# One row group of an encoder kernel: a second turn of its rows in the rounded type, compared with the full turn

## The chip, the cores and the metric

The kernel runs on one core of one Trainium2 chip. The metric is the device time of one execution in microseconds (us), from the first to the last work of the core. Times of before are the median of three executions and their lowest and highest. One further execution was taken by the hardware profiler; it has a time of its own, and all durations below come from it.

## The reference, cut to what matters

Two sequences of 1024 rows of 1024 channels, `x_prompt` and `x_sample`, go through one layer and a last norm. All is in float32.

```python
h = rmsnorm(x, g_mix) * (1.0 + sc1) + sh1
z = h @ w_in
q_lat, kv_lat, k_pe, f_in = z[..., :o1], z[..., o1:o2], z[..., o2:o3], z[..., o3:]
y_mla = mla_group(q_lat, kv_lat, k_pe, ...)
y_four = fourier_group(f_in, w_four)
x = x + ga1 * (jnp.concatenate([y_mla, y_four], axis=-1) @ w_out)
h2 = rmsnorm(x, g_ffn) * (1.0 + sc2) + sh2
x = x + ga2 * ((jax.nn.silu(h2 @ w_gate) * (h2 @ w_up)) @ w_down)
```

What the change touches is the first of these lines: the normed rows `x`, turned so that channels lie on the 128 partitions, and then scaled and shifted into `h`.

## The kernel before

**Stages.** The first stage, up to about 215 us, norms the rows of both sequences, turns them, projects them (`z = h @ w_in`, the Fourier columns folded with the cosine and sine tables), and writes latents to DRAM. It also folds small weights on the side. Attention and the Fourier part come next, up to about 740 us, and the rest is the feed-forward layer. Products of float32 values are made on TensorE (PE) as three products of split values: a value is split into a high part of the type `fp32r` and a low part that is the rest (`split`, L61 to L63: the high part by a copy on ACT, the low part by a subtraction on DVE), and `mm3` (L82 to L85) adds high times high, high times low and low times high.

**Row groups.** The first stage goes over eight groups `k` (`pairs`, L364), four for each sequence; a group is two row tiles `u` of 128 rows, `st1["x", k]`, each 128 x 1024. For a group, `norm` squares and scales the rows in place (L381 on ACT, `rstd` on POOL, L393 on DVE). `flip(k, g)` for g = 0 to 3 turns two channel tiles of both row tiles: `flip_t` makes four transposes on PE against the float32 identity `ident` into one PSUM bank (L409), and `flip_s` scales and shifts the bank into `hf` (L421 on ACT for k of 2 and more) and splits `hf` into `hh` and `hl`. The products that read `hh` and `hl` of group k + 1 come only in the next round.

**The place of the change.** `pair(k)` (L695) is one round. In round 2 stand, in this order in the code: the products of group 2 with `wz` for row tile 0 (`zproj`), whose bank is squared, given its reciprocal root and scaled into a tile `lat` (L490, L491 on DVE), the last 128 columns of it split into the tile `kv` (ACT and DVE) and sent to DRAM by two DMAs on SP's queue (L496, `ckv_d`); then `flip(3, 0)` and `flip(3, 1)`; then a piece of side work (L245 folds a weight, L222 multiplies the conditioning vector with a 1 MB block `wada` that SP loads with L215); then `zproj` for row tile 1.

**What sets the order.** A scheduler places the instructions on each engine's queue once, when the program is built. Each engine then takes its queue in that order, and an instruction that waits holds up all behind it. SP issues nearly all DMAs of this stage, also in order. PSUM has eight banks that go round (`bank`, tag `b`), and the SBUF tiles of tag `sk` (`stile`, L187) are three.

Of the kernel before, what the change touches and what calls it, by code (L numbers as in the profile page):

```python
# [13 lines left out]
F32R = mybir.dt.float32r  # L14
BF16 = mybir.dt.bfloat16
AF = mybir.ActivationFunctionType
ALU = mybir.AluOpType
# [4 lines left out]
P = 128  # L22
# [30 lines left out]
def hybrid_encoder_kernel(ctx: ExitStack, tc: tile.TileContext, a: dict):  # L53
    nc = tc.nc
# [3 lines left out]
    def rd(t):  # L58
        return t.bitcast(F32)

    def split(hi, lo, src):  # L61
        here["a"] = nc.scalar.copy(hi, src).ins  # L62
        here["v"] = nc.vector.tensor_tensor(out=lo, in0=src, in1=rd(hi), op=ALU.subtract).ins  # L63
# [29 lines left out]
    identr = const.tile([P, P], F32R, name="identr")  # L93
# [81 lines left out]
    with ExitStack() as st:  # L175
        p1b = st.enter_context(ExitStack())
        w2 = p1b.enter_context(tc.tile_pool(name="p1b", bufs=1, side="right", reuse_waits="tile"))
        w = st.enter_context(tc.tile_pool(name="p1", bufs=1, reuse_waits="tile"))
        pp = st.enter_context(tc.tile_pool(name="p1_ps", bufs=8, space=PSUM, reuse_waits="tile"))

        def bank():
            return pp.tile([P, 512], F32, tag="b", name="bank")
# [4 lines left out]
        def stile(name):  # L187
            return w.tile([P, 512], F32, tag="sk", name=name, bufs=3)
# [176 lines left out]
        st1 = {}  # L365
# [28 lines left out]

        def flip(k, g):
            flip_t(k, g)
            flip_s(k, g)

        def flip_t(k, g):
            if g == 0:  # L400
                st1["hf", k] = w2.tile([P, NC, 2, P], F32, tag="hf", name="hf", bufs=1)
                st1["hh", k] = w.tile([P, NC, 2, P], F32R, tag=f"hh{k % 2}", name="hh")
                st1["hl", k] = w.tile([P, NC, 2, P], F32R, tag=f"hl{k % 2}", name="hl")
            xt = st1["x", k]
            pt = bank().rearrange("p (c u t) -> p c u t", c=2, u=2)
            for c in range(2):
                for u in range(2):
                    cc = 2 * g + c
                    here["pe"] = nc.tensor.transpose(pt[:, c, u, :], xt[u][:, cc * P : (cc + 1) * P], ident).ins  # L409
            st1["pt", k, g] = pt  # L410

        def flip_s(k, g):
            s, j = pairs[k]
            hf, pt = st1["hf", k], st1.pop(("pt", k, g))
            for c in range(2):
                cc = 2 * g + c
                sc, sh = s1[s][:, cc : cc + 1], sh1[s][:, cc : cc + 1]
                if k < 2 and c == 1:
                    nc.vector.tensor_scalar(out=hf[:, cc], in0=pt[:, c], scalar1=sc, scalar2=sh, op0=ALU.mult, op1=ALU.add)
                else:  # L420
                    nc.scalar.activation(hf[:, cc], pt[:, c], AF.Identity, bias=sh, scale=sc)  # L421
            gs = slice(2 * g, 2 * g + 2)
            split(st1["hh", k][:, gs], st1["hl", k][:, gs], hf[:, gs])
# [271 lines left out]
        def pair(k, also=None):  # L695
# [22 lines left out]
            if k < nk - 1:  # L718
                flip(k + 1, 0)
                flip(k + 1, 1)  # L720
# [6 lines left out]
            if k + 1 < nk:  # L727
                flip(k + 1, 2)
                flip(k + 1, 3)
# [164 lines left out]
    with ExitStack() as st:  # L894
        early = st.enter_context(ExitStack())
        wa = early.enter_context(tc.tile_pool(name="p2a", bufs=1, reuse_waits="tile"))
        w = st.enter_context(tc.tile_pool(name="p2", bufs=1, side="right", reuse_waits="tile"))
        pp = st.enter_context(tc.tile_pool(name="p2_ps", bufs=8, space=PSUM, reuse_waits="tile"))
# [174 lines left out]
        for s in range(2):  # L1073
            for n in range(8):
                g, j = n // 4, (1, 2, 3, 0)[n % 4]
# [100 lines left out]
    with ExitStack() as st:  # L1176
        w = st.enter_context(tc.tile_pool(name="p3", bufs=1, side="right", reuse_waits="tile"))
        pp = st.enter_context(tc.tile_pool(name="p3_ps", bufs=1, space=PSUM, reuse_waits="tile"))
# [112 lines left out]
        for k in range(nit + 4):  # L1291
# [7 lines left out]
            if k < nit:  # L1299
                s, b, h, u = items[k]  # L1300
# [34 lines left out]
    with ExitStack() as st:  # L1335
        w = st.enter_context(tc.tile_pool(name="p5", bufs=1, reuse_waits="tile"))
# [150 lines left out]
        pp = st.enter_context(tc.tile_pool(name="p5_ps", bufs=8, space=PSUM, reuse_waits="tile"))  # L1487
# [19 lines left out]
        for s in range(2):  # L1507
# [78 lines left out]
            for n, f in enumerate(order):  # L1586
# [55 lines left out]
                x, y, z = bank(), bank(), bank()  # L1642
# [332 lines left out]
```

## Time and profile before

| | |
|---|---|
| median of 3 executions | 2033.69 us (2029.91 to 2034.99) |
| the profiled execution's own time | 2032.84 us |
| its span, first to last instruction | 2031.1 us |
| time around the span | 1.74 us |
| mean granted TensorE clock | 0.995 of full speed |
| DMA over the span | 370.33 MB, mean 182 GB/s |

The profile names instructions by their line in the kernel and by tiles, output first. "x8" behind a row means eight such instructions in a row. A duration in a timeline is that of the whole merged row, and the bracket at its end gives the idle time of the engine before it and what ended it. Matmuls overlap one another, so the distance between the starts of rows says more of PE's pace than the durations. PEclk is the clock that TensorE was granted, 1.00 at full speed.

### The profile page before, as it was taken

What the parts mean: (1) busy time and instruction counts of PE and PEld (TensorE: products, weight loads), DVE (VectorE), ACT (ScalarE), POOL (GpSimd) and SP (SyncE); (2) the same over time, 40 slices, a digit from 0 to 9 for tenths busy, and PEclk for the clock granted to TensorE, in tenths of its full rate; (3) what the DMA queues carried; (4) which work ended last, traced back from release to release, by engine and by line L of the source; (5) the groups of instructions that cost most, each with busy time, mean ns of one, the idle gap of its engine ahead of it and who ended that gap; (6) DMA issues with size and microseconds to landing.
All of it is one profiled execution on the core that took longest, in us unless ns stands there. A gap on an engine that the chain in (4) does not pass through costs nothing.

```text
span 2031.1 us, 28284 instructions
## 1 busy us (share of the span) xinstructions
PE 1985.5 (98%) x9840; PEld 1621.9 (80%) x9840; DVE 1405.3 (69%) x2088; ACT 896.3 (44%) x1733; POOL 824.3 (41%) x1013
## 2 busy tenths in 40 slices
PE   8899999999999999999999999999999999999997
PEld 7788777888787777888888888877788888888876
DVE  5667658766676679878677577687765656657674
ACT  4565545555554564333333365453333333336451
POOL 2454112112213227879778411233655554510142
PEclk9999999999999999999999999999999999999999
DMA  9695883445544475555555597664422322357772
GB/s 377 209 292 171 264 329 109 121 99 139 130 115 145 136 263 188 201 166 194 200 171 193 170 310 249 215 233 145 141 93 102 116 93 103 113 188 265 230 225 90
DMA packets 181963, 370.33 MB, mean 182 GB/s; under 512 B 18556, under 2 KB 58236, under 8 KB 177724
## 3 DMA queue, kind: packets, MB, share of 16 engines
q1 hardware_dynamic: 163148, 310.71, 45.9%
q0 software_dynamic: 18672, 57.81, 9.5%
q8 instruction: 77, 1.26, 0.3%
q14 instruction: 66, 0.54, 0.1%
HBM read 256.46 MB, written 120.39 MB: 186 GB/s over the span
## 4 chain that ended last, share of the span: by engine, by line
PE 51%; DMA 3%; DVE 3%; issue 1%; POOL 1%; ACT 1%; SPq 1%; DVEq 0%; ACTq 0%; POOLq 0%
PE bank L84 17%; PE bank L83 17%; PE bank L85 17%; DVE wl L63 1%; DMA val<-x_d 1%; DMA H<-s_d 1%; ACT wh L62 1%; DMA draw<-s_d 1%; POOL val L143 1%; DVE val L143 1%; DMA draw<-t_d 0%; DVE val L1772 0%; SPq L1732 0%; SPq L1731 0%; POOL rs_y L110 0%
## 5 line engine op out<-in xcount | busy, mean ns | idle before, releaser
L83 PE MATMUL bank<-H,wh 128*128 128x512 f32 x1224 | 477.4, 390 | 5.4 <-DVE val L143 4.8
L85 PE MATMUL bank<-H,wl 128*128 128x512 f32 x1224 | 476.4, 389 | 0.2 <-DVE wl L63 0.2
L84 PE MATMUL bank<-H,wh 128*128 128x512 f32 x1224 | 476.3, 389 | 0.0
L143 DVE TENSOR_TENSOR val<-bank,val 128x512 f32<-128x512 f32 x244 | 166.6, 688 | 170.6 <-PE bank L85 167.7
L83 PEld LDWEIGHTS bank<-H,wh 128*128 128x128 f32 x1224 | 229.8, 188 | 56.7 <-DVE val L143 7.1
L85 PEld LDWEIGHTS bank<-H,wl 128*128 128x128 f32 x1224 | 229.8, 188 | 49.4 <-DVE wl L63 1.5
L84 PEld LDWEIGHTS bank<-H,wh 128*128 128x128 f32 x1224 | 229.8, 188 | 47.3
L63 DVE TENSOR_TENSOR wl<-draw,wh 128x512 fp32r<-128x512 f32 x286 | 201.2, 738 | 83.4 <-ACT wh L62 82.9
L62 ACT CAST wh<-draw 128x512 fp32r<-128x512 f32 x286 | 168.7, 620 | 159.5 <-PE bank L84 84.5
L84 PE MATMUL bank<-wl,wh 128*128 128x512 f32 x572 | 223.8, 391 | 3.1 <-DVE wl L63 2.7
L143 POOL TENSOR_TENSOR val<-val 128x512 f32<-128x512 f32 x58 | 82.6, 1431 | 347.8 <-DVE val L1746 188.8
L85 PE MATMUL bank<-wh,wl 128*128 128x512 f32 x572 | 222.6, 389 | 0.0
L83 PE MATMUL bank<-wh 128*128 128x512 f32 x572 | 222.6, 389 | 0.0
L62 ACT CAST wh<-rgu 128x512 fp32r<-128x512 f32 x171 | 106.3, 623 | 251.0 <-PE bank L84 196.0
L63 DVE TENSOR_TENSOR wl<-val,wh 128x512 fp32r<-128x512 f32 x133 | 134.1, 1010 | 74.4 <-ACT wh L62 74.4
L63 DVE TENSOR_TENSOR wl<-rgu,wh 128x512 fp32r<-128x512 f32 x171 | 164.1, 960 | 7.6 <-ACT wh L62 7.6
L62 ACT CAST wh<-val 128x512 fp32r<-128x512 f32 x133 | 82.3, 622 | 178.8 <-PE bank L84 162.9
L140 POOL TENSOR_TENSOR val<-rgu 128x512 f32<-128x512 f32 x80 | 113.3, 1417 | 97.5 <-DMA rgu<-in_wgu_dram 93.8
L84 PEld LDWEIGHTS bank<-wl,wh 128*128 128x128 f32 x572 | 107.4, 188 | 29.2 <-DVE wl L63 7.2
L83 PEld LDWEIGHTS bank<-wh 128*128 128x128 f32 x572 | 107.4, 188 | 22.4
L85 PEld LDWEIGHTS bank<-wh,wl 128*128 128x128 f32 x572 | 107.4, 188 | 22.0
L140 POOL TENSOR_TENSOR val<-val 128x512 f32<-128x512 f32 x89 | 119.2, 1358 | 1.3
(393 smaller groups left out, 3910.6 us busy)
## 6 DMA issues: line engine op xcount, KB each, us to landing
rgu<-in_wgu_dram SPq DMA_DIRECT2D x86, 512.0 KB
draw<-s_d SPq DMA_DIRECT2D x143, 256.0 KB
s_d<-val POOLq DMA_DIRECT2D x88, 256.0 KB, 3.8
draw<-t_d SPq DMA_DIRECT2D x88, 256.0 KB
s_d<-val SPq DMA_DIRECT2D x66, 256.0 KB
wada<-in_wa_dram SPq DMA_DIRECT2D x16, 1024.0 KB
draw<-in_w_down_dram SPq DMA_DIRECT2D x55, 256.0 KB
xt<-in_x_dram SPq DMA_DIRECT2D x16, 512.0 KB
```

The source lines that it names most:

```text
L62: here["a"] = nc.scalar.copy(hi, src).ins
L63: here["v"] = nc.vector.tensor_tensor(out=lo, in0=src, in1=rd(hi), op=ALU.subtract).ins
L83: nc.tensor.matmul(out, lh, rh, start=first, stop=False, skip_group_check=cont)
L84: nc.tensor.matmul(out, lh, rl, start=False, stop=False, skip_group_check=cont)
L85: here["pe"] = nc.tensor.matmul(out, ll, rh, start=False, stop=last, skip_group_check=cont).ins
L140: return eng.tensor_tensor(out=out, in0=x, in1=y, op=ALU.subtract).ins
L143: return eng.tensor_tensor(out=out, in0=x, in1=y, op=ALU.add).ins
```

## The change

`flip(3, 0)`, one of 24 calls of `flip`, does more between its transposes and its scaling. The parts of both row tiles that it turns (256 channels each) are copied by two DMAs into a tile `xr` of the type fp32r. Four transposes against `identr`, the identity in fp32r, turn `xr` into a second bank `pr`. DVE then copies `pr` into a tile `d`, subtracts the bank of the full turn, multiplies by 1048576 and adds the full turn again. `flip_s` reads `d` in the place of the bank. What is computed is therefore the full turn plus 1048576 times the difference between the two turns; where the fp32r turn hands on the same values, that is the full turn itself.

```diff
         def flip(k, g):
             flip_t(k, g)
+            if (k, g) == (3, 0):
+                xr = w.tile([P, 512], F32R, tag="sk", name="xr", bufs=3).rearrange("p (c u t) -> p c u t", c=2, u=2)
+                pr = pp.tile([P, 512], F32R, tag="b", name="pr").rearrange("p (c u t) -> p c u t", c=2, u=2)
+                for u in range(2):
+                    nc.sync.dma_start(rd(xr)[:, :, u, :], st1["x", k][u][:, : 2 * P].rearrange("p (c t) -> p c t", c=2))
+                for c in range(2):
+                    for u in range(2):
+                        nc.tensor.transpose(pr[:, c, u, :], xr[:, c, u, :], identr)
+                d = stile("d").rearrange("p (c u t) -> p c u t", c=2, u=2)
+                nc.vector.tensor_copy(d, rd(pr))
+                nc.vector.tensor_tensor(out=d, in0=d, in1=st1["pt", k, g], op=ALU.subtract)
+                nc.vector.tensor_scalar(out=d, in0=d, scalar1=1048576.0, scalar2=None, op0=ALU.mult)
+                nc.vector.tensor_tensor(out=d, in0=d, in1=st1["pt", k, g], op=ALU.add)
+                st1["pt", k, g] = d
             flip_s(k, g)
```

The lines behind the inserted ones carry numbers that are 14 higher: L409 becomes L423 and L496 becomes L510. The added lines are L401 (the DMAs), L404 (the transposes) and L406 to L409 (the four steps on DVE). The scheduler places them as follows. Outside of the first stage the order of all five engines is what it was.

PE's queue in round 2 of before, from the last product of `zproj` for row tile 0 on; `bank<-ident,xt` are the eight transposes of `flip(3, 0)` and `flip(3, 1)`, and the bracket names the semaphores that a row waits for:

```order
L85 MATMUL bank<-wz_h,hl 128x448
L409 MATMUL bank<-ident,xt 128x128 [waits DVE_49,PE_49]
L409 MATMUL bank<-ident,xt 128x128 [waits DVE_49]
L409 MATMUL bank<-ident,xt 128x128 x6
L245 MATMUL bank<-wukT,zraw 128x128 x2
L222 MATMUL bank<-wada,scT 32x512 [waits DMAHW6_49]
```

The same place of PE's queue in the change:

```order
L423 MATMUL bank<-ident,xt 128x128 [waits DVE_49,PE_49]
L423 MATMUL bank<-ident,xt 128x128 [waits DVE_49]
L423 MATMUL bank<-ident,xt 128x128 x2
L404 MATMUL pr<-identr,xr 128x128 [waits DMAHW0_49]
L423 MATMUL bank<-ident,xt 128x128
L404 MATMUL pr<-identr,xr 128x128 [waits DMAHW1_49]
L404 MATMUL pr<-identr,xr 128x128 x2
L423 MATMUL bank<-ident,xt 128x128 x3
L245 MATMUL bank<-wukT,zraw 128x128 [waits PE_49]
L245 MATMUL bank<-wukT,zraw 128x128
L222 MATMUL bank<-wada,scT 32x512 [waits DMAHW6_49]
```

The four new transposes stand in the midst of the eight old ones, behind the fourth and the fifth of them, and two of them wait for DMAs.

SP's queue at the same place of before: the two DMAs of `kv` of group 2, row tile 0, the store of a folded weight, the load of the next `wada`, and the `kv` of row tile 1:

```order
L496 DMA ckv_d_93<-kv 128x128 [waits DMAHW6_49,Activation_49]
L496 DMA ckv_d_94<-kv 128x128 [waits DMAHW7_49,DVE_49]
L251 DMA wq_d<-zraw 256x1x512 [waits DMAHW0_49]
L215 DMA wada<-in_wa_dram 128x2048 [waits DMAHW1_49,PE_49]
L496 DMA ckv_d_93<-kv 128x128 [waits DMAHW2_49,Activation_49]
```

And of the change:

```order
L510 DMA ckv_d_93<-kv 128x128 [waits DMAHW6_49,Activation_49]
L510 DMA ckv_d_94<-kv 128x128 [waits DMAHW7_49,DVE_49]
L401 DMA xr<-xt 128x2x128 [waits DMAHW0_49,Pool_49]
L401 DMA xr<-xt 128x2x128 [waits DMAHW1_49]
L215 DMA wada<-in_wa_dram 128x2048 [waits DMAHW2_49,PE_49]
L251 DMA wq_d<-zraw 256x1x512 [waits DMAHW3_49,DVE_49]
```

The two new DMAs stand right behind the pair of `kv`, and the load of `wada` and the store of the folded weight have changed places behind them.

DVE's queue of before there, from the scaling of `lat` on:

```order
L491 TENSOR_SCALAR lat<-bank,rs_r 128x128
L247 SCALAR_TENSOR_TENSOR zraw<-bank,vecs,gkvr 128x128 [waits PE_49]
L247 SCALAR_TENSOR_TENSOR zraw<-bank,vecs,gkvr 128x128
L63 TENSOR_TENSOR hl<-hf,hh 128x512 [waits Activation_49]
L63 TENSOR_TENSOR kv<-lat,kv 128x128 [waits DMAHW2_49,DMAHW1_49,Activation_49]
L63 TENSOR_TENSOR hl<-hf,hh 128x512 [waits Activation_49]
```

And of the change:

```order
L505 TENSOR_SCALAR lat<-bank,rs_r 128x128
L63 TENSOR_TENSOR kv<-lat,kv 128x128 [waits DMAHW2_49,DMAHW1_49,Activation_49]
L406 COPY d<-pr 128x512 [waits PE_49]
L407 TENSOR_TENSOR d<-d,bank 128x512 [waits DVE_49]
L408 TENSOR_SCALAR d<-d 128x512 [waits DVE_49]
L247 SCALAR_TENSOR_TENSOR zraw<-bank,vecs,gkvr 128x128 [waits PE_49]
L409 TENSOR_TENSOR d<-d,bank 128x512 [waits DVE_49]
L63 TENSOR_TENSOR hl<-hf,hh 128x512 [waits Activation_49]
```

The subtraction that makes `kv` has come forward to stand right behind `lat`, and the four new steps stand behind it.

## The prediction

> **What bounds the kernel now.** I read the page's head first, then TensorE's waits, then the busy time by stretches around the place of the change.
>
> ```profile
> span 2031.1 us, 28284 instructions
> ...
> PE 1985.5 (98%) x9840; PEld 1621.9 (80%) x9840; DVE 1405.3 (69%) x2088; ACT 896.3 (44%) x1733; POOL 824.3 (41%) x1013
> ```
>
> PE is busy for 98% of the span, and no other engine is near that. A share over the span says little of one place, so next come the stretches. The columns are the stretch, its length, the busy time of each engine, PEclk, the DMA share and GB/s.
>
> ```profile
> 93.00:101.00 8.00, 8.00 (x51) 6.58 (x50) 5.42 (x12) 4.88 (x15) 3.71 (x10) 1.00 0.65 250
> 101.00:108.00 7.00, 7.00 (x57) 5.02 (x55) 3.35 (x9) 6.34 (x18) 3.73 (x10) 1.00 0.89 294
> 108.00:130.00 22.00, 22.00 (x127) 18.97 (x128) 15.16 (x32) 13.35 (x33) 11.61 (x26) 1.00 0.88 286
> 130.00:230.00 100.00, 98.91 (x627) 85.67 (x626) 74.40 (x166) 56.72 (x148) 43.74 (x97) 1.00 0.65 204
> ```
>
> From 93 to 130 us PE has no idle time at all, and from 130 to 230 us it has 1.1 us. So work that is added to PE here, or a time in which PE waits here, has next to nothing in the following 137 us that could take it up. All else in the stage has room: DVE works 5.42 of 8 us, ACT 4.88.
>
> **The change part by part: the wait.** These are PE's rows at the place.
>
> ```profile
> 93.01 1.03 PE L409 MATMUL bank<-ident,xt 128*128 128x128 f32 x8
> 93.88 0.61 PE L245 MATMUL bank<-wukT,zraw 128*128 128x128 f32 x4
> 94.42 1.06 PE L222 MATMUL bank<-wada,scT 128*32 128x512 f32 x8
> 95.42 0.47 PE L83 MATMUL bank<-wz_h,hh 128*128 128x448 f32 x1
> ...
> 100.22 0.37 PE L85 MATMUL bank<-wz_h,hl 128*128 128x448 f32 x1
> ```
>
> The eight transposes of `flip(3, 0)` and `flip(3, 1)` start 0.11 us apart (0.87 us from the first to the next row), so the fourth is issued by 93.45 us. In the change the first transpose of `xr` is next, and it waits for a DMA that SP issues behind the two DMAs of `kv`. So the question is when `kv` of this row tile is ready.
>
> ```profile
> 96.58 0.48 DVE L490 TENSOR_SCALAR lat<-bank,rs_r 128x256 f32<-128x256 f32 x1 [1.79 <-POOL rs_r L114]
> 96.99 0.34 DVE L491 TENSOR_SCALAR lat<-bank,rs_r 128x128 f32<-128x128 f32 x1
> ...
> 98.36 1.38 DVE L63 TENSOR_TENSOR kv<-lat,kv 128x128 fp32r<-128x128 f32 x1
> 97.36 0.30 ACT L62 CAST kv<-lat 128x128 fp32r<-128x128 f32 x1 [1.14 <-DVE lat L491]
> 97.69 2.41 SPq L496 DMA_DIRECT2D ckv_d<-kv  x2
> 99.77 0.33 SPq L496 DMA_DIRECT2D ckv_d<-kv  x1
> L63 DVE TENSOR_TENSOR kv<-lat,kv x8: 278/444/1380, 62.2 to 128.7; 128x128 fp32r<-128x128 f32 x8
> ```
>
> The chain is the reciprocal root on POOL, `lat` on DVE until 97.33 us, the high part of `kv` on ACT until 97.66 us, and the low part on DVE. Nothing in it waits for what follows on PE, so it keeps its times while PE stands. The low part is made earlier than before, since it now stands right behind `lat`: 97.66 us and 0.28 us (the minimum of eight; its 1.38 us here is the longest) are 97.94 us. The second `ckv_d` is then issued at about 98.0 us instead of 99.77, the first DMA of `xr` after its 0.33 us at 98.4, and the second, after 0.5 us, at 98.9.
>
> No row shows a copy of this kind from issue to landing. The nearest is the second `ckv_d` itself, half as large; the other end is the page's row for a store of 256 KB.
>
> ```profile
> 99.50:100.40 0.90, 0.90 (x6) 0.80 (x5) 0.84 (x2) 0.00 (x0) 0.09 (x1) 1.00 0.00 0
> 100.40:101.00 0.60, 0.60 (x7) 0.57 (x6) 0.00 (x0) 0.37 (x3) 0.00 (x0) 1.00 0.36 109
> ...
> s_d<-val POOLq DMA_DIRECT2D x88, 256.0 KB, 3.8
> ```
>
> Issued at 99.77 us, the small store leaves the DMA engines at 0.00 until 100.4 us and is then seen in the next 0.6 us, so it takes about 1.2 us. Bounds are therefore 0.9 us and 3.8 us; nearest to the small store I take 1.8 us for twice its bytes and the signal. The second half of `xr` lands at 98.9 + 1.8 = 100.7 us.
>
> At 93.45 us PE had four transposes left. At 100.7 us it has three of `xr` and three of the old ones left, since one of each fits between the two landings. The shift is 100.7 - 93.45 = 7.25 us, and two more transposes of 0.12 us: **7.5 us**. The fp32r transposes are priced like the old ones; a row for the same operation, `pqt` against `identr`, has nearly the same duration.
>
> ```profile
> L859 PE MATMUL pqt<-identr,qsk x64: 222/248/281, 299.3 to 662.4; 128*128 128x128 f32 x64
> ```
>
> **The clock behind the wait.** A stop of 7 us does not only cost itself.
>
> ```profile
> 18.78:22.18 3.40, 2.22 (x34) 1.72 (x35) 2.63 (x4) 0.00 (x0) 0.24 (x2) 0.50 1.04 421
> 22.20:25.59 3.39, 3.39 (x18) 3.39 (x17) 0.91 (x5) 0.56 (x1) 0.00 (x0) 0.50 0.99 408
> 70.00:73.38 3.38, 0.16 (x4) 0.00 (x0) 2.33 (x4) 2.51 (x7) 1.46 (x2) 1.00 0.00 0
> 73.40:76.79 3.39, 3.17 (x12) 2.49 (x12) 1.38 (x8) 2.92 (x11) 1.99 (x6) 0.50 0.88 244
> 640.00:643.40 3.40, 1.48 (x9) 0.64 (x7) 3.40 (x4) 0.90 (x2) 3.40 (x3) 1.00 0.02 5
> 643.42:646.82 3.40, 3.40 (x15) 3.32 (x16) 1.95 (x4) 2.31 (x7) 2.26 (x3) 0.50 0.28 33
> ```
>
> Twice PE was idle for much of a stretch of 3.4 us (busy for 0.16 us from 70.00, for 1.48 us from 640.00), and each time the granted clock was 0.50 in the next one. The first pair of rows shows how long that can last: with 2.22 of 3.40 us busy from 18.78 us at 0.50, a second stretch stayed at 0.50; from 73.40 us, with 3.17 busy, one was enough. The wait here is longer than any of these gaps. One stretch of 3.4 us at half rate does 1.7 us less work: **1.7 us**, with 0.85 (PE comes back in the middle of a stretch) and 3.4 (two stretches) as bounds.
>
> [...]
>
> **What lies beside other work.** The four steps on DVE cost some 0.7 us each.
>
> ```profile
> 123.92 0.67 DVE L227 COPY modrow<-bank 128x512 f32<-128x512 f32 x1
> 97.25 0.60 DVE L247 SCALAR_TENSOR_TENSOR zraw<-bank,vecs,gkvr 128x128 f32<-128x128 f32 x2
> ```
>
> Four such and one L247 of 0.3 us make 3.0 us, from the last transpose of `xr` at about 101 us to some 104.5 us with the slower clock. While DVE stands before the copy, from 98 to 101 us, it holds up L247 and `hl`, for which no one waits in that time. ACT then scales `d` and splits it until about 106 us. The products for row tile 1 of group 2, 95.42 to 100.43 us before, come to stand at 104 to 110 us and need none of this. The next transposes that need a bank which `d` frees come behind these products. If that cover were gone, the 3 us would be added. The load of `wada` waits for L222, which moves along, and it now goes ahead of the 512 KB of `wq_d`; its reader moves along too. Two DMAs of 128 KB each take little from a stage whose DMA share is 0.65 here, and they fall into a time when PE has stopped and asks for no loads.
>
> **The sum.** 7.5 + 1.7 = 9.2 us on the profiled execution's own 2032.84 us (span 2031.1) is **2042.0 us**. That execution stands 0.85 us under the median of 2033.69, so against the median it is 8.3 us or 0.41% more. The ends: with a landing after 0.9 us, 0.85 us of clock and the one later wait of PE for a load regained (below), 5.7 us, 2038.5; with a landing after 3.8 us and 3.4 us of clock, 12.9 us, 2045.7. The three runs of before spread from -3.8 to +1.3 us about their median, for which I add 1.5 us on each side.
>
> **The rivals.** *Not slower: the copies leave early.* The rows of group 3 are normed long before.
>
> ```profile
> 87.22 1.42 DVE L393 TENSOR_SCALAR xt<-xt,rs_r 128x1024 f32<-128x1024 f32 x2 [0.61 <-POOL rs_r L114]
> ```
>
> From 88.64 us both copies could go. If they did, they would land by 88.64 + 0.5 + 3.8 = 92.9 us, before PE comes to them at 93.45 us; only four transposes of 0.12 us would be left, and the time would be 2033.3 us. The point from which it decides is whether SP has the DMAs of `kv` ahead of them. The order says it has, and SP issues in order. I see no way round that: 5%.
>
> *Regained later.* The wait could be taken back where PE waits for something that doesn't move with it.
>
> ```profile
> PE bank L1062 <- DMA wada<-in_w_ada_dram: 1.8, 1, 1.8
> PE bank L505 <- DVE lat L490: 1.1, 1, 1.1
> PE bank L83 <- DVE ed L143: 1.1, 1, 1.1
> ```
>
> Of PE's waits up to 300 us behind this place, only the first ends by a DMA; the others end by DVE, whose work follows on PE's. All three gone would be 4.0 us, 2038.0 us. That is within 0.3% of before. Against it: these loads are issued where PE frees their tiles, so they move along. 8%.
>
> *Longer.* Two slow stretches and a landing near 3.8 us, or a second stop where the 3 us on DVE come out from under the products, give 2045 to 2047.5 us. The products of 5 us speak against the stop. 8%.
>
> *The change doesn't do what it says.* If both turns are equal, the difference is zero. No instruction goes away for that, so there is no other time in it.
>
> **How the numbers follow.** The forecast, a wait of 6 to 9 us that stays, has 79%, and a small part of it, 4%, ends under the bound of 0.3% (6.1 us, about what a measurement can tell from no change). Slower is 75 + 8 = 83%; the same is 4 + 8 and most of the early copies, 15%; faster is left with 2%. The range takes in the ends with the spread, 2037.0 to 2047.5 us.
>
> **What would show it.** In the profile of after, the row of L404 should have an idle time of about 7 us that ends by a DMA of `xr`, the two DMAs of L401 should start behind those of `ckv_d` at about 98 to 99 us, PEclk should be 0.50 in a stretch of some 3 us from about 97 to 104 us, and PE should be without gaps from there to 130 us. L404 without idle time, or the second stop at L423 or L83 behind it, would prove the sum wrong; so would waits that are gone later on.

## The result, and the profile after

| | before | after |
|---|---|---|
| median of 6 executions each | 2034.79 us (2029.91 to 2038.12) | 2044.15 us (2042.04 to 2047.32) |
| ratio to before, 95% interval | | 1.0052 (1.0041 to 1.0063) |
| the profiled execution's own time | 2032.84 us | 2043.35 us |
| its span | 2031.1 us | 2041.6 us |
| mean granted TensorE clock | 0.995 | 0.992 |

The changed kernel is slower by 0.52%, 10.6 us with an interval of 8.3 to 12.8 us. The forecast was 2042.0 us, and the range 2037.0 to 2047.5 us.

The busy time of each engine from the head of the page of after:

```profile
PE 1989.1 (97%) x9844; PEld 1623.8 (80%) x9844; DVE 1418.9 (69%) x2092; ACT 897.7 (44%) x1733; POOL 829.5 (41%) x1013
```

PE was given four instructions and 3.6 us of busy time, but the span grew by 10.5 us. So PE stood still more than before. Its list of waits has a new row at the top (the waiting instruction, what it waited for, us in all, times, longest), and a row that was in the prediction has shrunk:

```profile
PE pr L404 <- DMA xr<-xt: 6.9, 1, 6.9
...
PE bank L1076 <- DMA wada<-in_w_ada_dram: 0.7, 1, 0.7
```

PE's timeline at the place (start, duration of the merged row, instruction, idle time before it):

```profile
93.99 0.60 PE L423 MATMUL bank<-ident,xt 128*128 128x128 f32 x4
101.53 0.37 PE L404 MATMUL pr<-identr,xr 128*128 128x128 f32 x1 [6.95 <-DMA xr<-xt]
101.70 0.43 PE L423 MATMUL bank<-ident,xt 128*128 128x128 f32 x1
102.17 0.62 PE L404 MATMUL pr<-identr,xr 128*128 128x128 f32 x3
102.59 0.86 PE L423 MATMUL bank<-ident,xt 128*128 128x128 f32 x3
103.25 1.06 PE L245 MATMUL bank<-wukT,zraw 128*128 128x128 f32 x4
104.24 1.89 PE L222 MATMUL bank<-wada,scT 128*32 128x512 f32 x8
106.05 0.47 PE L83 MATMUL bank<-wz_h,hh 128*128 128x448 f32 x1
```

The rows of L245 and L222 stand in before too, but there they are twice as dense: L245 now takes 0.99 us to the next row instead of 0.54, L222 1.81 instead of 1.00.

**A measure for all kernels below.** From the first of the eight old transposes to the first product behind L222, before has 95.42 - 93.01 = 2.41 us. What a kernel has more than that between the same two rows is called its *loss at the place*. It leaves out what executions differ by ahead of the place, which is 0.98 us here (93.99 against 93.01). In after it is 106.05 - 93.99 - 2.41 = 9.65 us.

The busy time by stretches (stretch, length, PE, PEld, DVE, ACT, POOL, PEclk, DMA share, GB/s) shows both of its parts:

```profile
95.70:99.10 3.40, 0.00 (x0) 0.00 (x0) 1.04 (x3) 0.30 (x1) 1.72 (x7) 1.00 0.62 252
99.12:102.50 3.38, 0.93 (x5) 0.64 (x5) 0.00 (x0) 0.00 (x0) 0.00 (x0) 0.50 0.39 116
102.50:105.90 3.40, 3.40 (x18) 1.71 (x16) 3.00 (x6) 1.95 (x4) 0.00 (x0) 0.50 0.02 5
...
115.00:139.00 24.00, 24.00 (x145) 20.18 (x145) 14.87 (x31) 15.29 (x37) 13.49 (x27) 1.00 0.79 255
```

PE does nothing in a whole stretch of 3.4 us, and then the clock is 0.50 in two such stretches. The first of the two lies mostly under the wait; the second is all work at half rate. Later, from 115 to 139 us, PE is at full clock and never idle, as in before.

Why PE waited so long is on SP and DVE (SPq is the queue that SP issues DMAs from):

```profile
98.33 0.81 SPq L510 DMA_DIRECT2D ckv_d<-kv  x2
98.34 0.29 DVE L63 TENSOR_TENSOR kv<-lat,kv 128x128 fp32r<-128x128 f32 x1 [0.36 <-ACT kv L62]
102.83 0.69 DVE L406 COPY d<-pr 128x512 f32<-128x512 f32 x1 [4.20 <-PE pr L404]
...
104.88 0.68 DVE L409 TENSOR_TENSOR d<-d,bank 128x512 f32<-128x512 f32 x1
```

The group of the two copies by tile has their least, middle and longest time of issue in ns, and their first and last start:

```profile
L401 SPq DMA_DIRECT2D xr<-xt x2: 612/630/647, 99.2 to 99.9; - x2
```

The rows that the copies read had been ready for some 10 us (L393 was over by 88.64 us before), but SP issues in order, and ahead of the copies stand the two DMAs of `kv`, which wait for `lat` and its split. The copies start at 99.2 and 99.9 us, and the transposes that wait for them run at 101.53 and 102.17 us, 2.3 us behind each issue. DVE's four steps follow under the products.

### The profile page after: what moved, and what is told of

It is laid out like the page before. It is cut to its first block, busy times and chain, and to the rows that moved or that the text cites. A ratio compares the mean times of both kernels' runs of the same rounds, so it can differ in the third digit from the quotient of the medians.

```text
span 2041.6 us, 28307 instructions
## 1 busy us (share of the span) xinstructions
PE 1989.1 (97%) x9844; PEld 1623.8 (80%) x9844; DVE 1418.9 (69%) x2092; ACT 897.7 (44%) x1733; POOL 829.5 (41%) x1013
## 4 chain that ended last, share of the span: by engine, by line
PE 55%; DVE 2%; DMA 2%; POOL 1%; issue 1%; ACT 0%; SPq 0%; DVEq 0%; ACTq 0%; POOLq 0%
PE bank L84 18%; PE bank L83 18%; PE bank L85 18%; DVE wl L63 1%; DMA val<-x_d 1%; DMA draw<-s_d 1%; POOL val L143 1%; DVE val L143 0%; DMA draw<-t_d 0%; ACT wh L62 0%; DVE val L1786 0%; POOL rs_y L110 0%; DVE val L1760 0%; SPq L1745 0%; DVE val L1775 0%
```

## The experiments

The theory on trial is that of the prediction: the loss is a wait of PE for two copies held up on SP, and the half clock behind it; the four steps on DVE and the traffic of the copies cost nothing. The rivals: the steps on DVE are what costs, or the copies cost by being there at all, wherever they stand. The medians of before in these comparisons were 2033.64 to 2034.03 us.

**1. Without the four DVE steps.** This kernel leaves out the difference; the second turn is made and not read.

```diff
-                d = stile("d").rearrange("p (c u t) -> p c u t", c=2, u=2)
-                nc.vector.tensor_copy(d, rd(pr))
-                nc.vector.tensor_tensor(out=d, in0=d, in1=st1["pt", k, g], op=ALU.subtract)
...
-                st1["pt", k, g] = d
```

> Leaves out the four steps on DVE; the scaling reads the full turn as before, and what the second turn gives is not used. Theory (PE stands for the two copies, 7.5 us, and runs some 2 us behind at half clock): 9 to 10.5 us more than before, L404 with about 7 us of idle time that ends by a DMA of xr. Rival (the steps on DVE make the time): 0 to 3 us more than before.

Measured: 1.0058 (1.0038 to 1.0077). PE at the place:

```profile
95.68 0.60 PE L417 MATMUL bank<-ident,xt 128*128 128x128 f32 x4
103.20 0.37 PE L404 MATMUL pr<-identr,xr 128*128 128x128 f32 x1 [6.92 <-DMA xr<-xt]
...
107.42 0.47 PE L83 MATMUL bank<-wz_h,hh 128*128 128x448 f32 x1
```

The loss is 107.42 - 95.68 - 2.41 = 9.33 us with no DVE work of the change in it. The steps on DVE aren't the cause.

**2. The DVE steps alone.** No copies and no second turn: `d` is copied from the full turn, so the difference is that of a value with itself.

```diff
-                xr = w.tile([P, 512], F32R, tag="sk", name="xr", bufs=3).rearrange("p (c u t) -> p c u t", c=2, u=2)
-                pr = pp.tile([P, 512], F32R, tag="b", name="pr").rearrange("p (c u t) -> p c u t", c=2, u=2)
...
-                        nc.tensor.transpose(pr[:, c, u, :], xr[:, c, u, :], identr)
                 d = stile("d").rearrange("p (c u t) -> p c u t", c=2, u=2)
-                nc.vector.tensor_copy(d, rd(pr))
+                nc.vector.tensor_copy(d, st1["pt", k, g])
```

> Keeps the four steps on DVE, but on the full turn itself: no copies, no second turn, the difference is zero by construction. Theory: 0 to 1 us more than before, no new gap on PE. Rival (DVE): 5 to 10 us more.

Measured: 0.9994 (0.9985 to 1.0004). PE at the place:

```profile
92.42 1.03 PE L416 MATMUL bank<-ident,xt 128*128 128x128 f32 x8
...
94.83 0.47 PE L83 MATMUL bank<-wz_h,hh 128*128 128x448 f32 x1
```

94.83 - 92.42 is 2.41 us, to the last digit that of before. With run 1 this puts all of the loss on the copies and the second turn.

**3. The copies ahead of `kv`.** They are issued ahead of `zproj` for row tile 0, so nothing of `kv` stands ahead of them on SP.

```diff
             else:
+                if k == 2:
+                    xr = w.tile([P, 512], F32R, tag="sk", name="xr", bufs=3).rearrange("p (c u t) -> p c u t", c=2, u=2)
+                    for u in range(2):
+                        nc.sync.dma_start(rd(xr)[:, :, u, :], st1["x", 3][u][:, : 2 * P].rearrange("p (c t) -> p c t", c=2))
+                    st1["xr"] = xr
                 zproj(k, 0)
```

> The two copies are issued ahead of the DMAs of kv, but behind the loads of wada (1 MB) and of the next rows (2 x 512 KB), at about 92 us; all else as in the change. If the place on SP's queue alone sets the wait, they land at about 94.5 us and the change costs 1 to 2 us. If the copies also have to go through the 2 MB ahead of them, which keep the DMA engines busy until about 98 us, they land at 98 to 99.5 us, PE stands for 5 to 6 us, and it costs 6.5 to 9 us.

Measured: 1.0040 (1.0026 to 1.0055), the second of the two cases that were expected. The timeline of SP and PE, and the stretch behind the issue:

```profile
90.06 0.57 SPq L215 DMA_DIRECT2D wada<-in_wa_dram  x1
90.68 0.93 SPq L371 DMA_DIRECT2D xt<-in_x_dram  x2
91.71 1.41 SPq L729 DMA_DIRECT2D xr<-xt  x2
...
93.21 0.60 PE L421 MATMUL bank<-ident,xt 128*128 128x128 f32 x4
98.87 0.37 PE L402 MATMUL pr<-identr,xr 128*128 128x128 f32 x1 [5.06 <-DMA xr<-xt]
...
103.17 0.74 PE L83 MATMUL bank<-wz_h,hh 128*128 128x448 f32 x1
```

```profile
91.70:97.90 6.20, 2.11 (x13) 1.70 (x11) 2.93 (x8) 2.17 (x7) 3.81 (x10) 0.97 1.00 349
```

The copies were issued 7.5 us earlier than in after (91.71 against 99.23; counted from the first old transpose, 6.7 us earlier), but PE was let go only 98.87 - 91.71 = 7.16 us behind the issue, where after has 2.3 us. Ahead of them on SP stand the 1 MB of `wada` and two loads of `xt` of 512 KB each, and the DMA engines were busy all the time (share 1.00). So being ahead of `kv` isn't enough: the loss is 103.17 - 93.21 - 2.41 = 7.55 us, and half clock again. PEclk is 0.50 from 97.90 to 104.00 us here, so the slow clock reaches past the product that the measure ends at; up to the transposes of `lat` (108.72 us here, 100.43 in before) the loss is 8.09 us.

**4. The copies ahead of those loads.** The same lines as in run 3 now stand right behind the norm of group 3, in round 1.

```diff
             if k + 2 < nk:
                 norm(k + 2)
+            if k == 1:
+                xr = w.tile([P, 512], F32R, tag="sk", name="xr", bufs=3).rearrange("p (c u t) -> p c u t", c=2, u=2)
...
+                st1["xr"] = xr
```

> The two copies are issued as soon as the rows are normed, at about 88.7 us, ahead of those 2 MB. Theory: they land by 92 us, L404 has no idle time, the clock stays at 1.00, and four transposes are left: 0.3 to 1.5 us more than before. Rival (transposes, banks or steps on DVE make the time): still 5 to 10 us more.

Measured: 1.0001 (0.9990 to 1.0012). SP and PE:

```profile
88.44 1.31 SPq L747 DMA_DIRECT2D xr<-xt  x2
...
92.59 0.77 SPq L215 DMA_DIRECT2D wada<-in_wa_dram  x1
93.41 1.26 SPq L371 DMA_DIRECT2D xt<-in_x_dram  x2
...
95.25 0.60 PE L421 MATMUL bank<-ident,xt 128*128 128x128 f32 x4
95.61 0.54 PE L402 MATMUL pr<-identr,xr 128*128 128x128 f32 x4
...
97.98 0.47 PE L83 MATMUL bank<-wz_h,hh 128*128 128x448 f32 x1
```

No idle time, and a loss of 97.98 - 95.25 - 2.41 = 0.32 us, which four transposes of 0.1 us explain. All of the change is in this kernel, its DVE steps and its 256 KB of copies too. What costs time in after is only when the copies leave.

**5. Work in the wait, to hold the clock.** Multiplications of `ident` by itself, whose result no one reads, stand ahead of the transposes of `xr`; `spin` is a helper that the kernel has for its start.

```diff
+                here["pe0"] = here["pe"]
+                with tc.issue_after(here["pe"]):
+                    spin(60)
                 for c in range(2):
                     for u in range(2):
-                        nc.tensor.transpose(pr[:, c, u, :], xr[:, c, u, :], identr)
+                        with tc.issue_after(here["pe"]):
+                            nc.tensor.transpose(pr[:, c, u, :], xr[:, c, u, :], identr)
```

> 60 multiplications of the identity by itself (128 x 128, float32, about 0.11 us each, 6.6 us) fill PE's wait ahead of the first transpose of xr; their result isn't used. Theory (wait 7.5 us plus 2 us of half clock): the clock stays at 1.00 around the place, the rows behind it come 7 to 8 us later than in before, and the loss is 7 to 8 us. Rival (the clock takes nothing, all of it is the wait): 9 to 10 us as in the change.

Measured: 1.0075 (1.0060 to 1.0090); a miss of mine in the size, as PE's timeline shows.

```profile
95.51 13.56 PE L631 MATMUL bank<-ident 128*128 128x128 f32 x120
108.83 0.54 PE L408 MATMUL pr<-identr,xr 128*128 128x128 f32 x4
```

The 60 multiplications are 120 starts, 0.111 us apart (108.83 - 95.51 over 120), 13.3 us in all, longer than the wait they were to fill. The run says nothing of the clock's price; run 6 takes half as many.

**6. Half as much work in the wait.** `spin(30)` in place of `spin(60)`.

> As the run with 60 multiplications, with 30: each float32 multiplication of the identity took two starts of 0.111 us there, so 60 of them were 13.3 us and longer than the wait; 30 are 6.7 us and end about 1 us ahead of the landing. Theory (wait of some 7.5 us plus half clock): PEclk stays at 1.00 around the place, the rows behind it are 7.2 to 8.0 us later than ahead of it, measured against the rows of before, in place of 9.7 us in the change. Rival (the clock takes nothing there): 9 to 10 us.

Measured: 1.0046 (1.0031 to 1.0060). PE and SP at the place, and the stretch behind the wait:

```profile
95.67 0.60 PE L427 MATMUL bank<-ident,xt 128*128 128x128 f32 x4
96.10 6.86 PE L631 MATMUL bank<-ident 128*128 128x128 f32 x60
101.63 1.31 SPq L401 DMA_DIRECT2D xr<-xt  x2
103.92 0.28 PE L408 MATMUL pr<-identr,xr 128*128 128x128 f32 x1 [0.96 <-DMA xr<-xt]
...
106.44 0.47 PE L83 MATMUL bank<-wz_h,hh 128*128 128x448 f32 x1
```

```profile
103.00:106.00 3.00, 2.08 (x20) 1.44 (x20) 0.96 (x3) 1.26 (x3) 0.00 (x0) 1.00 0.28 83
```

Now PEclk is 1.00 behind the wait, and from the first transpose of `xr` to the product takes 106.44 - 103.92 = 2.52 us, where after has 106.05 - 101.53 = 4.52. The loss of 106.44 - 95.67 - 2.41 = 8.36 us is over my 7.2 to 8.0 us because the wait itself was longer in this execution: the copies were issued 101.63 - 95.67 = 5.96 us behind the first old transpose, in after 99.23 - 93.99 = 5.24, since the second store of `kv` ahead of them took 1.11 us to issue, in after 0.38. That is 0.72 us; without it the loss would be 7.64 us. Of the 2.0 us that are then left to after, some 0.3 us are not the clock: in this kernel all four old transposes run between the first and the second of `xr` and cover the second landing, in after only one does. This reading rests on one trace of each kernel: the ratios alone, 1.0046 and 1.0052, do not tell the two apart.

**7. The second turn later on PE.** The four old transposes and the copies stay where they are, but the transposes of `xr`, the DVE steps and the scaling of `flip(3, 0)` come behind `zproj` for row tile 1.

```diff
             if k < nk - 1:
-                flip(k + 1, 0)
+                if k == 2:
+                    flip_t(3, 0)
...
+                    st1["xr"] = xr
+                else:
+                    flip(k + 1, 0)
                 flip(k + 1, 1)
...
             if k > 1:
                 zproj(k, 1)
+            if k == 2:
+                with tc.issue_after(here["pe"]):
+                    flip(3, 0)
```

> The copies stay where they are on SP's queue; the four transposes, the steps on DVE and the scaling of these rows come behind the products of row tile 1 (5 us of PE). Theory: the products and the rows of side work cover the wait, PE has at most 1 us of idle time there, and 0.5 to 2 us are left over before. Rival (the copies or the work cost the time wherever PE takes them): 5 to 10 us.

Measured: 1.0019 (1.0010 to 1.0028). Two rows of PE:

```profile
102.10 0.25 PE L403 MATMUL pr<-identr,xr 128*128 128x128 f32 x1 [0.55 <-DMA xr<-xt]
...
114.03 0.47 PE L85 MATMUL bank<-wz_h,hl 128*128 128x448 f32 x1 [0.84 <-DVE hl L63]
```

The 5 us of products cover most of the wait: 0.55 us is left, and the clock doesn't fall: the eight of L222 behind it take 104.95 - 103.95 = 1.00 us, as in before. But the DVE steps now stand ahead of readers that are near, and a product with `wz_h` waits 0.84 us for `hl`, where before has no wait. This fits the cover of DVE's 3 us that the prediction named: here part of it is gone. What I can point to is 0.55 and 0.84 us and the four transposes of 0.11 us, 1.8 us. From the first old transpose to the eight of the next group the trace has 118.61 - 93.98 us, before 115.42 - 93.01, which is 2.22 us more. The ratio says 3.9 us (2.0 to 5.7), and both are over the 0.5 to 2 us expected. The profiled execution, 2033.77 us, is the shortest of its ten (median 2037.43), so what the others lose beyond this does not show in the trace and stays open.

**8. The same change at a second place.** `flip(5, 0)` gets it too.

```diff
-            if (k, g) == (3, 0):
+            if (k, g) in ((3, 0), (5, 0)):
```

> The same block also for flip(5, 0). Theory: a second wait of 6 to 8 us and half clock behind it, 17 to 21 us more than before in all. Rival (a loss of one time only, or one that later waits take back): 10 to 13 us.

Measured: 1.0092 (1.0076 to 1.0109). The second place on PE, its stretches, and the same part of PE's timeline in before:

```profile
150.85 0.60 PE L423 MATMUL bank<-ident,xt 128*128 128x128 f32 x4
155.22 0.37 PE L404 MATMUL pr<-identr,xr 128*128 128x128 f32 x1 [3.77 <-DMA xr<-xt]
...
165.59 0.60 PE L519 MATMUL bank<-ident,lat 128*128 128x128 f32 x4
```

```profile
154.65:158.00 3.35, 2.78 (x10) 2.18 (x11) 2.16 (x5) 1.76 (x4) 0.75 (x3) 0.50 0.15 45
158.05:161.40 3.35, 3.35 (x7) 1.81 (x6) 3.10 (x6) 1.00 (x3) 0.00 (x0) 0.50 0.00 1
```

```profile
138.93 1.04 PE L409 MATMUL bank<-ident,xt 128*128 128x128 f32 x8
...
146.42 0.60 PE L505 MATMUL bank<-ident,lat 128*128 128x128 f32 x4
```

From the first old transpose to those of `lat` it is 165.59 - 150.85 = 14.74 us, before 146.42 - 138.93 = 7.49: a second loss of 7.25 us. Its wait is only half as long, 3.77 us where 6 to 8 were expected, but the clock costs more than at the first place, since PE comes back early in the first slow stretch: of 6.7 us at 0.50 it works 6.13, which is 3.1 us lost. With the wait and four transposes of 0.11 us that is the 7.25 us. The first place, from 94.87 to 106.90 us, has a loss of 9.62 us as in after. Both together are 16.9 us, and the ratio says 18.7 us (15.5 to 22.2).

## Why the prediction was right

**The wait.** The step was that SP holds the copies behind `kv`, and that PE stands for them in the midst of the old transposes. Both are in the rows of after, and runs 3 and 4 show that the time at which the copies leave and land is all of it: with the copies landed in time the whole change costs 0.32 us. In the prediction's own count, the second landing sets the term. It put the issue of the second copy 98.9 - 93.01 = 5.9 us behind the first old transpose; it was 99.9 - 93.99 = 5.9 us. `kv` came forward as the order said: the making of its low part began at 98.34 us, 4.35 us behind the first old transpose, where the prediction had 97.66 - 93.01 = 4.65. That the two issues agree to the digit is luck: `kv` was 0.3 us early, and from its end to the second issue it took 99.93 - 98.63 = 1.3 us, where the prediction had 98.9 - 97.94 = 1.0. The landing was mis-sized: 1.8 us taken from a store of half the size, 2.3 us measured. The four old transposes take 0.44 us to issue, up to 94.43 us. So the term is 102.17 - 94.43 = 7.7 us and the two further transposes, **8.0 us against 7.5**.

**The clock.** From the second landing to the product, at full clock, six transposes of 0.11 us, L245 and L222 take 2.2 us; they took 106.05 - 102.17 = 3.88. That is **1.7 us against 1.7**, and the stretch from 102.50 us, 3.40 us of work at half rate, shows where. Run 6 has the same work at full clock (PEclk 1.00 from 103.00 to 106.00 us). What I had not put right is the number of slow stretches: two, not one, of which the first cost next to nothing here because the wait lay over it. So the same 1.7 us came from another course of events, and that they agree is in part luck. My lower bound of 0.85 us, for a return in the midst of a stretch, had it the wrong way round: in after, in run 3 and at the second place of run 8 PE came back in the midst of a slow stretch, and each time a second slow one followed: after has 0.93 us of work in the first 3.38 us, run 8 2.78 in 3.35, and in run 3 PE came back at 98.87 us and the clock stayed at 0.50 up to 104.00 us.

The stretch in which PE came back cost 1.4 us at the second place of run 8 (half of 2.78 us), where 3.1 us were lost in all, and next to nothing in after, where it was mostly idle.

**DVE, and the copies' traffic.** Both were put at nothing, hidden beside the products for row tile 1. Run 2 has the steps and no loss, run 1 the loss without the steps, run 4 the copies with no loss. Run 7 shows the price of the steps when part of their cover is gone: 0.84 us.

**The sum and the rivals.** 8.0 + 1.7 gives 9.65 us with the roundings, against 9.2. The other 0.98 us of the profiled execution lie ahead of the place, in code that is the same. Against the median the forecast was 8.3 us or 0.41% more, and 0.52% was measured. The upper end of the range lies 0.3 us above its own sum (2045.7 + 1.5 = 2047.2 us). *Regained later*: the one wait for a DMA that the rival named is still there but fell from 1.8 to 0.7 us, about a quarter of the 4.0 us priced; the other two rows are as long as before. In runs 2 and 4, with next to no loss, this wait was 1.3 and 2.0 us, so the small gain may be real. But ahead of it PE lost as much and more, in two waits that before does not have there; a third row shows what was left of it (first and last start at the end of the figures):

```profile
PE bank L519 <- DVE lat L505: 0.4, 1, 0.4
PE bank L83 <- DVE ll L63: 1.4, 1, 1.4
L873 PE MATMUL pqt<-identr,qsk x64: 222/249/284, 310.9 to 674.6; 128*128 128x128 f32 x64
```

The two waits stand at 140.46 and 232.94 us. Runs 1 and 3 have both of them too, runs 2 and 4 neither; how they come about was not followed. The first and the last of the `pqt` rows start 11.6 and 12.2 us later than in before (299.3 and 662.4), which is more than the 10.6 us behind the place, and the span is 10.5 us longer. Where it gets back the last 1.7 us was not looked for either. *The copies leave early*: they didn't, and the point from which I let it decide was not enough. I wrote that it decides whether SP has `kv` ahead of the copies; run 3 has no `kv` ahead of them and still loses 7.55 us, with 2 MB of loads ahead on the same queue. My price for it, 3.8 us at most from issue to landing, was too low there: from the first issue to its reader it was 7.16 us. Only run 4 is the rival as it was meant, and it ends where the rival said, at no change. *Longer*: the landing stayed far from 3.8 us, and there was no second stop at the steps on DVE (the later wait of 1.4 us is in run 1 too, which has no such steps); the median of 2044.15 us is a little under that rival's 2045 to 2047.5 us.

## What to carry to other kernels

What the small copies cost in this full pipeline was set by what stood ahead of them on their issuing queue: PE stood 6.95 us for them behind stores that waited (after), 5.06 us behind 2 MB of loads that were still moving (run 3), and not at all when they left ahead of both (run 4). So look at when a copy's source is ready, and issue it there, ahead of the next large loads. The stops of TensorE of 3.77 to 6.95 us in after and runs 1, 3 and 8 had half clock behind them, a second price: 1.7 us in after, and 3.1 us at the second place of run 8, where 6.13 us of work fell into the slow stretches. If such a stop can't go, move independent products into it: with multiplications in the stop, run 6 kept PEclk at 1.00. And before a helper's work is called hidden, name what hides it: the same DVE steps cost nothing ahead of 5 us of products and 0.84 us behind them.

## What the runs showed of the hardware that was not expected

The copy of 128 KB from `xt` to `xr` took 2.3 us from issue to the reader's start with only two stores of 64 KB right ahead of it, and 7.16 us behind 2 MB of loads issued up to 1.7 us before it on the same queue.

A float32 multiplication of 128 x 128 by 128 x 128 makes two starts in the trace of run 5, 0.111 us apart (120 for 60); a float32 transpose of that size makes one (the four of L423 in after are a row of x4).

The slow stretch at about 72 us, in code that the change doesn't touch, lasts longer in after than in before, where it was the stretch of 3.39 us from 73.40 us that the prediction shows:

```profile
71.90:82.00 10.10, 7.88 (x32) 7.20 (x33) 7.38 (x21) 8.15 (x24) 5.85 (x12) 0.50 0.91 259
```

It is 10.1 us here, and the first old transpose of the place starts at 93.99 us, in before at 93.01 us. Over the ten profiled executions that start lies between 92.42 us (run 2) and 95.68 us (run 1). So the difference of two profiled spans carries up to some 3 us that are not the change's, which is why the runs were compared by the loss at the place and by medians.

How much work in a stretch goes with which clock in the next can be counted in the traces of before and after, where PEclk changes only on a grid of 3.41 us (counted from 10 to 2010 us). Of 1157 such windows at full clock, all 7 in which PE was busy for up to 0.44 of the window were followed by half clock, and none of the 1150 with 0.46 or more. Of the 11 windows at half clock, all four with up to 0.80 were followed by another one, the one with 0.81 and all six with 0.93 or more by full clock. At the second place of run 8 a stretch with 0.83 (2.78 of 3.35 us) was followed by another slow one.
